# A fused decoder block on one core: inputs of a job in attention split one every two steps, operand of the exchange on VectorE, the last class of keys split at the end of a slot

## The chip, the core and the metric

The kernel runs on one core of one Trainium2 chip, as one program in one launch. The core's engines are TensorE (PE in the profile, its weight loads PEld), VectorE (DVE), ScalarE (ACT), GpSimd (POOL) and SyncE (SP). Each engine executes its own instructions strictly in program order; an instruction that waits holds up all that stand behind it on the same engine. SP and ACT also issue the DMAs, so a DMA that waits for its buffer, too, holds up its queue. The metric is the device time of one execution in microseconds (us): the median of several executions.

## The reference

One layer of a decoder block on a sequence of 2048 tokens with 1024 channels, all in float32:

```python
mod = c_act @ w_mod[l] + b_mod[l]
shift, scale, gate = jnp.split(mod, 3, axis=-1)
h = rms_norm(x, g_norm[l]) * (1.0 + scale[:, None, :]) + shift[:, None, :]
proj = h @ w_in[l]
x_rnn, z_rnn, q, k, v, z_attn, g_r, g_a = jnp.split(proj, IN_SPLITS, axis=-1)
xc = causal_depthwise_conv(x_rnn, conv_w[l], conv_b[l])
hr = rg_lru(xc, w_a[l], b_a[l], w_x[l], b_x[l], lam[l], positions)
y_rnn = (hr * jax.nn.silu(z_rnn)) @ w_out_rnn[l]
qh, kh = apply_partial_rope(q), apply_partial_rope(k)
o = dilated_attention_mixture(qh, kh, vh).reshape(B, S, D_ATTN)
y_attn = (o * jax.nn.silu(z_attn)) @ w_out_attn[l]
merged = sigmoid(g_r + bg_r) * y_rnn + sigmoid(g_a + bg_a) * y_attn
x = rms_norm(x + gate * (merged @ w_o[l]), g_final)
```

The attention has 8 heads of 128 channels. It is evaluated with three causal windows (128 keys at dilation 1, 512 at dilation 4, 2048 at dilation 16) whose results are merged by their softmax denominators.

## The kernel before

Every large product is done in float32 accuracy with three passes of a cheaper type: each operand is **split** into a high part (a copy rounded to the type `fp32r`) and a low part (the rest), and `mm3` issues high x high, high x low and low x high. So each operand costs a copy (`hi_act` on ACT or `hi_dve` on DVE) and a subtraction (`lo_pool` on POOL or `lo_dve` on DVE) before TensorE can use it.

The program goes through these stages; the times are those of the profiled execution.

- **Prologue** (0 to about 57 us): `x` is normalised and turned, 8 MB of `w_mod` are loaded and reduced to shift and scale; then the first products of the values run. Where TensorE would have nothing to do, `idle_matmuls(n)` issues n matmuls on a constant tile (`busy`).
- **Values** of a half of the tokens (`values_half(f, xs)`; for f = 0 to about 124 us, for f = 1 to about 787 us). `wide_values` runs the products of four groups; each call of `next` on it issues a quarter of a group. `store_values` then evicts a finished PSUM tile on ACT (`ev`, L855). Between them, calls of `next(odd)` advance `build_odd`, a generator of twelve steps which makes the split operands `B12`, `B22` and T1 to T4 that the next stage needs (sums on DVE, high parts on ACT, low parts on DVE; `t` and `hx` are its temporaries). How many calls stand where sets the place of these instructions in the queues of ACT and DVE.
- **Strassen stage** of a half (to about 697 us and 1346 us): the other columns of `w_in`, multiplied in seven products (X, Z, W, V, X, Y, V) per pair. The rotated and plain queries and keys are stored in DRAM (`qT`, `kT`; L1160, L1192).
- **Attention** (about 1346 to 1890 us): 16 heads (8 heads for each half of the tokens) in six units each, `ORDER`: class `c` 0 to 3 (the four residues of the positions modulo 4) and window `w` 0 and 1. A unit takes a **slot**. In a slot the program issues, in this order: what is planned at HEAD, the scores of the unit on TensorE, its softmax (minimum on DVE, L1485; exponential on ACT, L1486), what is planned at SOFTMAX, EXCHANGE and WEIGHTS, the transposes of the unit seven slots before, the sums of the one eight slots before, and what is planned at TAIL. Between these, `spend` issues steps of `steps(jobs)`: the output projections (`pj`), which fill TensorE while the softmax chain runs.
- A head's queries and keys are loaded per class (`load_kq`, into `kraw`, 4 buffers) and split into the single tile `KQ` (`split_kq`: `kq`). `window_queries` rearranges the queries (`q`, on POOL). After a head's six units, `gather` puts the softmax minima and sums into `sm` (four ACT instructions, L1638), `exchange` multiplies it by a constant on TensorE (into a PSUM tile with the tag `sc`, as the scores), and `maxima`, `exponentials` and `weights` make from it the scale of each unit. `enlist` holds the slots: class 3 is loaded at the end of slot B - 3 and split at the head of slot B, where B is the first slot of its head.
- A **job** of the filling work multiplies one quarter of the tokens by one output projection, in 64 steps of three matmuls. Its eight inputs are loaded and split by the tables `LOAD_Y` and `SPLIT_Y`, by step x, where steps 8 to 15 are the first eight of the job, each using one input. `split_y` puts the low parts on POOL or DVE (`yl`). The weights `S<-wD` are loaded in the same order on SP. The eight inputs of the first job are split at once before attention.
- **End** (1890 to 2179 us): the remaining jobs, the last product with `w_o`, and the final norm.

Inside `tc.manual_schedule()` the instructions stand in each engine's queue as the code issues them (strassen stage, attention, end, most of the prologue); the values are outside of it and are ordered by the framework's scheduler. A DMA also waits until the DMA eight places before it has landed (each takes one of eight semaphores in turn).

## Time and profile before

| what | value |
| --- | --- |
| median of 3 runs | 2180.11 us (2179.24 to 2183.7) |
| the profiled execution, and its span from first to last instruction | 2180.94 us, 2179.2 us |
| TensorE's idle time over the span | 34.1 us (2179.2 - 2145.1) |
| idle TensorE from 100 to 200 us, and its mean clock there | 3.6 us, 0.97 |
| idle TensorE from 200 to 1300 us | 1.9 us |
| idle TensorE from 1300 to 1900 us | 12.2 us |
| idle TensorE from 2100 us to the end | 10.2 us |

In the profile, `out<-in` names what an instruction writes and reads, and a bracket behind a row says how long the engine was idle before it and what ended this. Two matmuls of 512 columns start 0.23 us apart at full clock. DMA busy is the mean share of the 16 DMA engines.

### The profile page before, as it was taken

The page shows a single profiled execution, that of the slowest core. Times are in us where ns is not written, and L with a number is a line of the kernel's source. Part 1 is how long each engine was busy: PE and PEld are TensorE (multiplying, and loading weights), DVE is VectorE, ACT ScalarE, POOL GpSimd, SP SyncE. Part 2 cuts the span into 40 slices and gives each one's busy share as a digit, 9 for nine tenths or more (in the row PEclk, how much of TensorE's full clock was granted, in tenths as well). Part 3 has the DMA queues.
Part 4 walks back from the last instruction along what each step waited for, and adds up shares of the span by engine and source line. Part 5 has one row for each costly group of instructions (what it writes and reads, how often), then busy time and mean ns, then how long its engine had stood idle before and what let it go on. Part 6 is the DMA issues. An engine that isn't in the chain of part 4 may idle for free.

```text
span 2179.2 us, 32758 instructions
## 1 busy us (share of the span) xinstructions
PE 2145.1 (98%) x10564; PEld 1791.9 (82%) x10564; DVE 1483.5 (68%) x2564; ACT 1313.1 (60%) x2621; POOL 1075.2 (49%) x803
## 2 busy tenths in 40 slices
PE   9999999999999999999999999999999999999998
PEld 6878888888788888888888887888888988878886
DVE  6579877868656535545446584577777777688887
ACT  5648668668644537457447532677888887343333
POOL 1357677667666323223224665456666665200543
PEclk9999999999999999999999999999999999999999
DMA  8457887887655378899996666888887877898552
GB/s 302 141 202 255 281 299 270 288 287 240 174 112 164 110 247 284 291 312 310 322 330 214 164 160 194 287 251 253 279 262 222 259 236 239 291 314 296 179 174 107
DMA packets 426608, 522.98 MB, mean 240 GB/s; under 512 B 104166, under 2 KB 291778, under 8 KB 425412
## 3 DMA queue, kind: packets, MB, share of 16 engines
q1 hardware_dynamic: 391860, 421.06, 61.9%
q10 hardware_dynamic: 34384, 99.78, 12.3%
q8 instruction: 84, 1.38, 0.2%
q14 instruction: 88, 0.72, 0.1%
q0 software_dynamic: 192, 0.05, 0.0%
HBM read 332.02 MB, written 188.75 MB: 239 GB/s over the span
## 4 chain that ended last, share of the span: by engine, by line
PE 59%; DMA 6%; issue 2%; POOL 2%; ACT 2%; DVE 2%; SPq 1%; ACTq 0%; POOLq 0%; DVEq 0%
PE X L151 12%; PE V L151 11%; PE pj L151 10%; PE Z L151 6%; PE W L151 6%; PE Y L151 5%; PE o L151 3%; PE sc L151 3%; DMA S<-wD 1%; PE pg L151 1%; DMA kraw<-kT 1%; PE pT L1570 1%; DMA vraw<-vN 1%; PE pT L1583 1%; DMA R<-yaT 1%
## 5 line engine op out<-in xcount | busy, mean ns | idle before, releaser
L165 POOL TENSOR_TENSOR S<-R,S 128x512 fp32r<-128x512 f32 x192 | 293.2, 1535 | 182.6 <-ACT S L159 89.3
L151 PE MATMUL X<-T,S 128*128 128x512 f32 x1344 | 326.2, 392 | 4.7 <-ACT ev L855 3.6
L151 PE MATMUL pj<-yh,S 128*128 128x512 f32 x896 | 324.5, 403 | 2.3 <-DMA S<-wD 1.6
L151 PE MATMUL V<-T,S 128*128 128x512 f32 x1344 | 324.2, 390 | 0.2 <-DVE ev L454 0.2
L151 PEld LDWEIGHTS X<-T,S 128*128 128x128 f32 x1344 | 253.3, 189 | 59.2 <-ACT ev L855 4.0
L151 PEld LDWEIGHTS V<-T,S 128*128 128x128 f32 x1344 | 252.0, 188 | 53.8 <-DVE ev L454 0.7
L165 POOL TENSOR_TENSOR S<-s,S 128x512 fp32r<-128x512 f32 x116 | 172.2, 1484 | 144.9 <-ACT S L159 105.5
L151 PEld LDWEIGHTS pj<-yh,S 128*128 128x128 f32 x896 | 168.4, 188 | 32.6 <-DVE st L1485 2.0
L151 PE MATMUL pj<-yl,S 128*128 128x512 f32 x448 | 176.2, 393 | 1.9 <-POOL yl L165 1.4
L1486 ACT ACTIVATE pp<-pp,st 128x256 f32<-128x256 f32 (+3 forms) x256 | 133.5, 523 | 52.9 <-DVE st L1485 52.3
L159 ACT ACTIVATE S<-s 128x512 fp32r<-128x512 f32 x124 | 77.4, 624 | 142.7 <-DVE s L284 92.0
L151 PE MATMUL Z<-T,S 128*128 128x512 f32 x672 | 162.0, 390 | 0.0
L151 PE MATMUL Y<-T,S 128*128 128x512 f32 x672 | 161.8, 390 | 0.0
L151 PE MATMUL W<-T,S 128*128 128x512 f32 x672 | 161.6, 389 | 0.0
L159 ACT ACTIVATE S<-R 128x512 fp32r<-128x512 f32 x200 | 121.2, 621 | 60.1 <-issue 20.4
L168 DVE TENSOR_TENSOR ptl<-pT,pth 128x384 fp32r<-128x384 f32 (+1 forms) x160 | 97.8, 628 | 77.3 <-ACT pth L159 75.1
L151 PEld LDWEIGHTS W<-T,S 128*128 128x128 f32 x672 | 126.0, 188 | 26.9 <-issue 0.9
L151 PEld LDWEIGHTS Z<-T,S 128*128 128x128 f32 x672 | 126.1, 188 | 26.2
L151 PEld LDWEIGHTS Y<-T,S 128*128 128x128 f32 x672 | 125.9, 188 | 26.1
L974 DVE SCALAR_TENSOR_TENSOR xc<-xr,par,xc 128x512 f32<-128x512 f32 x96 | 103.6, 1079 | 54.9 <-ACT xc L968 52.7
L165 POOL TENSOR_TENSOR s<-R,s 128x512 fp32r<-128x512 f32 x32 | 44.1, 1378 | 187.8 <-ACT s L159 168.7
L1550 ACT ACTIVATE pp<-pp,M 128x256 f32<-128x256 f32 (+3 forms) x256 | 118.0, 523 | 9.6 <-DVE M L1673 9.6
(417 smaller groups left out, 4902.9 us busy)
## 6 DMA issues: line engine op xcount, KB each, us to landing
sD<-S ACTq DMA_DIRECT2D x140, 512.0 KB, 3.6
S<-sD SPq DMA_DIRECT2D x140, 512.0 KB, 5.0
S<-wD SPq DMA_DIRECT2D x82, 512.0 KB, 5.6
R<-in_w_in_dram SPq DMA_DIRECT2D x144, 256.0 KB, 3.6
wD<-s ACTq DMA_DIRECT2D x64, 256.0 KB, 5.1
T<-in_w_mod_dram SPq DMA_DIRECT2D x16, 512.0 KB, 8.9
vN<-ev SPq DMA_DIRECT2D x32, 256.0 KB, 2.7
zaT<-ev SPq DMA_DIRECT2D x32, 256.0 KB, 4.4
```

The lines of the kernel that those rows point to most:

```text
L151: nc.tensor.matmul(o, lhsT=l, rhs=r, start=st, stop=sp, **kw)
L159: nc.scalar.activation(o, i, AF.Copy)
L165: nc.gpsimd.tensor_tensor(o, i, h.bitcast(F32), ALU.subtract)
L168: return nc.vector.tensor_tensor(o, i, h.bitcast(F32), ALU.subtract).ins
L974: nc.vector.scalar_tensor_tensor(xc, xr[:, i : i + CH], cw(i), xc, ALU.mult, ALU.add)
L1486: nc.scalar.activation(pdst, pdst, AF.Exp, bias=m_, scale=-1.0, accum_out=l_)
L1550: nc.scalar.activation(pp, pp, AF.Copy, scale=w)
L1570: nc.tensor.transpose(pt[:, c0 + j * P : c0 + (j + 1) * P], pp[i][:, k * P : (k + 1) * P], ident)
L1583: nc.tensor.transpose(pt[:, c * P : (c + 1) * P], pp[:, half * P : (half + 1) * P], ident)
```

## The change

The change has seven parts.

1. The scratch tensors `qT` and `kT` become one, `kqT`, in which the queries of a half lie beside the keys that it uses. A class is loaded by one DMA in place of two, and for the first head the classes 1 to 3 are issued by ACT (before: class 3 alone).
2. `gather` is two `tensor_tensor` on DVE, with the mask broadcast, in place of four activations on ACT.
3. Class 3 is loaded one slot earlier and split at WEIGHTS of slot B - 1 in place of HEAD of slot B.
4. `SPLIT_Y` spaces the splits of inputs 1 to 6 by two steps; `LOAD_Y` is moved accordingly.
5. Of the first job's inputs, 6 and 7 have their low parts on DVE.
6. The prologue has seven more idle matmuls.
7. In `values_half` the calls of `next(odd)` stand earlier.

```diff
-    qT = scratch("qT", [D, 4, NB * P])
-    kT = scratch("kT", [D, 4, NB * P])
+    kqT = scratch("kqT", [D, 4, 2 * NB * P])
+    q_column = lambda n: (n if n < 2 else NB + n) * P
+    k_column = lambda n: (2 + n) * P
...
-        idle_matmuls(2)
-        last_sums(0, fill=1)
+        idle_matmuls(4)
+        last_sums(0, fill=2)
         modulation(0)
         hi_k(1)
         sums(1, 2)
         build_x(0)
         lo_k(1)
         turn_x(1)
+        idle_matmuls(3)
...
         for x, _ in enumerate(wide_values(vx, 1, n1, (1, 0), ws)):
-            if x == 0:
+            for _ in range((1, 2, 1, 0)[x]):
                 next(odd)
         with tc.issue_after(last_ev[0]):
             next(odd)
             next(odd)
-        for x, _ in enumerate(wide_values(vx, 0, n1, (0, 1))):
+        for _ in wide_values(vx, 0, n1, (0, 1)):
             next(odd, None)
-            if x == 0:
-                next(odd, None)
...
             self.nk = (self.bk[1] + 1) * P
+            self.q0, self.k0 = (self.nk, 0) if f else (0, 2 * P)
...
-            q0 = self.bk[0] * P
-            queue = nc.scalar if self.f == self.h == 0 and c == 3 else nc.sync
-            queue.dma_start(t[:, : self.nk], kT[rows, c, : self.nk])
-            queue.dma_start(t[:, self.nk : self.nk + 2 * P], qT[rows, c, q0 : q0 + 2 * P])
+            c0, w = self.f * 2 * P, self.nk + 2 * P
+            (nc.scalar if self.f == self.h == 0 and c else nc.sync).dma_start(t[:, :w], kqT[rows, c, c0 : c0 + w])
...
-            for q in range(4):
-                nc.scalar.activation(self.sm[:, :, q], self.st[:].rearrange("p t g b n -> p g t (b n)"), AF.Copy,
-                                     scale=qm[:, q : q + 1])
+            for g in range(2):
+                nc.vector.tensor_tensor(
+                    self.sm[:, g], self.st[:, :, g].rearrange("p t b n -> p t (b n)").unsqueeze(1).broadcast_to([P, 4, 2, 8]),
+                    qm.unsqueeze(2).unsqueeze(3).broadcast_to([P, 4, 2, 8]), ALU.mult)
...
-            for c, (ld, s, place) in enumerate(((5, 2, HEAD), (5, 2, SOFTMAX), (4, 1, HEAD), (3, 0, HEAD))):
+            for c, (ld, s, place) in enumerate(((5, 2, HEAD), (5, 2, SOFTMAX), (4, 1, HEAD), (4, 1, WEIGHTS))):
...
-                (lo_dve if j and k % 2 or j > NB + 1 else lo_pool)(yl[:], t[:], yh[:])
+                (lo_dve if (k % 2 if j else k > 5) or j > NB + 1 else lo_pool)(yl[:], t[:], yh[:])
...
-    LOAD_Y = {-12: [0], -10: [1], -8: [2], -6: [3], -2: [4], 4: [5], 5: [6], 6: [7]}
-    SPLIT_Y = {-3: [0], 3: [1], 4: [2], 5: [3], 7: [4], 10: [5], 11: [6], 12: [7]}
+    LOAD_Y = {-12: [0], -10: [1], -8: [2], -6: [3], -2: [4], 2: [5], 4: [6], 6: [7]}
+    SPLIT_Y = {-3: [0], 1: [1], 3: [2], 5: [3], 7: [4], 9: [5], 11: [6], 12: [7]}
```

What this does to the queues is shown at three places.

**ACT, end of the values of the first half.** The rows stand just ahead of the evictions `ev` of the last group; `T<-hx` and `T<-t` are high parts from `build_odd`, `S` those of the first operands of the strassen stage. Before:

```order
L159 ACTIVATE T_888<-hx_686 128x512
L159 ACTIVATE T_890<-hx_690 128x512
L159 ACTIVATE T_892<-t_206_1164 128x512
L278 DMA sD<-S_222_1246 128x1024
L159 ACTIVATE T_894<-t_197_1115 128x512
L159 ACTIVATE S_228_1262<-R_218_1236 128x512
L159 ACTIVATE S_226_1256<-s_219_1238 128x512
L855 ACTIVATE ev_1178<-W_1024 128x512
L159 ACTIVATE T_888<-hx_687 128x512
L855 ACTIVATE ev_1187<-X_1025 128x512
L159 ACTIVATE T_890<-hx_691 128x512
L855 ACTIVATE ev_1196<-V_1026 128x512
```

and now:

```order
L160 ACTIVATE T_898<-hx_699 128x512
L160 ACTIVATE S_225_1259<-R_217_1240 128x512
L160 ACTIVATE S_223_1254<-s_221_1247 128x512
L160 ACTIVATE T_902<-t_200_1139 128x512
L279 DMA sD<-S_223_1254 128x1024
L160 ACTIVATE S_229_1270<-R_219_1244 128x512
L160 ACTIVATE S_227_1264<-s_220_1246 128x512
L857 ACTIVATE ev_1194<-W_1056 128x512
L857 ACTIVATE ev_1203<-X_1057 128x512
L857 ACTIVATE ev_1212<-V_1058 128x512
L857 ACTIVATE ev_1221<-X_1059 128x512
```

No high part stands between the evictions any more: the last two of `hx` and the last of `t` have moved ahead of them. Behind the eviction of Z that precedes this stretch ACT has eight high parts of `build_odd` where it had thirteen, and DVE has fewer of its sums and low parts left there too.

**SP, start of attention.** The rows are the first head's loads and the weights of the filling work. Before:

```order
L1432 DMA kraw_12128<-kT 128x256
L1433 DMA kraw_12128<-qT 128x256
L1432 DMA kraw_12131<-kT 128x256
L1433 DMA kraw_12131<-qT 128x256
L1432 DMA kraw_12134<-kT 128x256
L1433 DMA kraw_12134<-qT 128x256
L339 DMA S_2258_12149<-wD 128x1024
L339 DMA S_2260_12168<-wD 128x1024
```

and now:

```order
L1432 DMA kraw_12136<-kqT 128x512
L340 DMA S_2259_12153<-wD 128x1024
L340 DMA S_2261_12172<-wD 128x1024
L1779 DMA fg_12183<-grT 128x512
L340 DMA S_2263_12193<-wD 128x1024
```

One load stands ahead of the weights where six stood; the other three are in ACT's queue, behind the high parts `yh<-T` of the first job and ahead of the first `kq<-kraw`.

**ACT, one slot with a gather** (a head of the second half; `pp` are the softmax tiles, `pth` the high parts of the transposed ones). Before:

```order
L1486 ACTIVATE pp_17537,st_17137<-pp_17537,st_17137 128x512
L1638 ACTIVATE sm_17547<-st_17137,cs_60 128x2x16 x4
L159 ACTIVATE pth_17557<-pT_17552 128x512
L159 ACTIVATE pth_17565<-pT_17561 128x384
L1550 ACTIVATE pp_17067<-pp_17067,M_17162 128x384
L1550 ACTIVATE pp_17067<-pp_17067,M_17162 128x512
L159 ACTIVATE vh_17592<-vraw_17451 128x512
L159 ACTIVATE kq_12082<-kraw_17453 128x768
```

and now:

```order
L1485 ACTIVATE pp_17465,st_17069<-pp_17465,st_17069 128x512
L160 ACTIVATE kq_12090<-kraw_17301 128x768
L160 ACTIVATE pth_17485<-pT_17480 128x512
L160 ACTIVATE pth_17493<-pT_17489 128x384
L1550 ACTIVATE pp_17001<-pp_17001,M_17094 128x384
L1550 ACTIVATE pp_17001<-pp_17001,M_17094 128x512
L160 ACTIVATE vh_17520<-vraw_17382 128x512
L1485 ACTIVATE pp_17541,st_17532<-pp_17541,st_17532 128x384
```

The four activations are gone from ACT, and the high part of class 3 stands where they stood. On DVE the two products `sm` stand behind the minima of the last unit and ahead of the low parts `ptl`. On POOL the low part of class 3 now precedes `vh` in the queue, and the copies `q` follow `vh`.

More of the change, by code (lines that the diff above doesn't have):

```diff
@@ L1122, in decoder_block @@
     NT0, NT1 = (4, 5), 3
-    QK = ((2 * D, qT, -SCALE), (3 * D, kT, 1.0))
+    QK = ((2 * D, q_column, -SCALE), (3 * D, k_column, 1.0))
     def scaled(t, ps, u, qs):
@@ L1136, in rotated_pairs, with rotated @@
     def rotated_pairs(qp, f, Ct, St):
-        for base, dstT, qs in QK:
-            def rotated(i, j, ps, u, dstT=dstT, qs=qs):
+        for base, column, qs in QK:
+            def rotated(i, j, ps, u, column=column, qs=qs):
                 n = 2 * f + j
@@ L1159, in store @@
                         r0 = (4 * i + hh) * P
-                        nc.sync.dma_start(dstT[r0 : r0 + 32, :, n * P : (n + 1) * P],
+                        nc.sync.dma_start(kqT[r0 : r0 + 32, :, column(n) : column(n) + P],
                                           v[0][hh * 32 : (hh + 1) * 32, :].rearrange("p (r j) -> p r j", r=4))
@@ L1181, in plain_pairs, with plain @@
     def plain_pairs(f):
-        for base, dstT, qs in QK:
+        for base, column, qs in QK:
             for t in range(0, 6, 2):
-                def plain(i, j, ps, u, t=t, dstT=dstT, qs=qs):
+                def plain(i, j, ps, u, t=t, column=column, qs=qs):
                     n = 2 * f + j
@@ L1191, in store @@
                         for p0, r0, m in cuts[t + i]:
-                            nc.sync.dma_start(dstT[r0 : r0 + m, :, n * P : (n + 1) * P],
+                            nc.sync.dma_start(kqT[r0 : r0 + m, :, column(n) : column(n) + P],
                                               t0[p0 : p0 + m, :].rearrange("p (r j) -> p r j", r=4))
@@ L1444, in window_queries @@
             for l in range(2):
-                src = KQ[:, l, :, self.nk + i * P : self.nk + (i + 1) * P].bitcast(F32)
+                src = KQ[:, l, :, self.q0 + i * P : self.q0 + (i + 1) * P].bitcast(F32)
                 copy = nc.gpsimd if self.f or self.h else nc.vector
@@ L1500, in scores_c @@
                 o0 = P if n == 1 else 0
-                q = slice(self.nk + i * P, self.nk + (i + 1) * P)
-                mm3(ps[:, o0 : o0 + w], KQ[:, 0, r, q], KQ[:, 1, r, q], KQ[:, 0, r, :w], KQ[:, 1, r, :w],
+                q = slice(self.q0 + i * P, self.q0 + (i + 1) * P)
+                ks = slice(self.k0, self.k0 + w)
+                mm3(ps[:, o0 : o0 + w], KQ[:, 0, r, q], KQ[:, 1, r, q], KQ[:, 0, r, ks], KQ[:, 1, r, ks],
                     first=n != 1, last=True, skip_group_check=True)
@@ L1515, in keys @@
         def keys(self, l, w0, nb):
-            ap = KQ[:, l, 0, w0 * 32 : w0 * 32 + 32]
+            ap = KQ[:, l, 0, self.k0 + w0 * 32 : self.k0 + w0 * 32 + 32]
             return bass.AP(ap.tensor, ap.offset, [list(ap.ap[0]), [32, nb], [KQW, 4], [1, 32]])
```

## The prediction

> **What bounds the kernel now.** I read the page's busy line first, then the busy times by stage, then TensorE's waits, then the timeline at the longest of them.
>
> ```profile
> PE 2145.1 (98%) x10564; PEld 1791.9 (82%) x10564; DVE 1483.5 (68%) x2564; ACT 1313.1 (60%) x2621; POOL 1075.2 (49%) x803
> ...
> 20.00:24.00 4.00, 4.00 (x11) 3.17 (x12) 3.96 (x7) 2.55 (x4) 0.00 (x0) 0.57 1.08 362
> 126.00:133.00 7.00, 5.23 (x12) 4.14 (x13) 6.06 (x7) 3.74 (x7) 3.38 (x2) 0.53 0.43 135
> 1346.00:1370.00 24.00, 21.45 (x102) 16.80 (x101) 8.49 (x26) 8.04 (x22) 7.94 (x7) 1.00 0.95 293
> 1370.00:1620.00 250.00, 245.91 (x1596) 217.28 (x1595) 175.16 (x557) 198.46 (x612) 152.44 (x148) 1.00 0.85 265
> 1620.00:1890.00 270.00, 264.81 (x1707) 235.87 (x1705) 195.34 (x470) 211.09 (x515) 156.55 (x121) 1.00 0.77 242
> ```
>
> TensorE is busy for 98% and sets the time; the change takes no matmul from it. So what there is to gain is its idle time, and the time at a low clock. The stage rows give the stretch, then the busy time of PE, PEld, DVE, ACT and POOL, the granted clock, DMA share and GB/s. The clock is about one half in two stretches alone. In attention TensorE idles 2.55 us at the start and 4.09 + 5.19 = 9.3 us behind it. Who ends it (first row: 124 to 1340 us; the others: 1370 to 1890 us; total, times, longest):
>
> ```profile
> PE X L151 <- ACT ev L855: 3.6, 1, 3.6
> ...
> PE sc L151 <- DVE st L1485: 2.3, 3, 1.7
> PE pT L1570 <- ACT pp L1550: 2.1, 6, 0.6
> PE pT L1570 <- DVE ptl L168: 1.4, 2, 0.7
> PE sc L151 <- POOL q L1447: 1.3, 2, 0.8
> PE pj L151 <- POOL yl L165: 0.8, 2, 0.6
> PE pj L151 <- DVE yl L168: 0.5, 1, 0.5
> ```
>
> **Part 7, first half: the eviction that comes late.**
>
> ```profile
> 122.67 1.52 PE L151 MATMUL X<-S,T 128*128 128x512 f32 x6
> 127.77 5.49 PE L151 MATMUL X<-T,S 128*128 128x512 f32 x12 [3.59 <-ACT ev L855]
> 135.90 2.88 PE L151 MATMUL W<-T,S 128*128 128x512 f32 x12
> ...
> 126.60 0.63 ACT L159 ACTIVATE T<-hx 128x512 fp32r<-128x512 f32 x1 [1.46 <-DVE hx L612]
> 104.52 0.60 ACT L855 ACTIVATE ev<-Z 128x512 f32<-128x512 f32 x1 [0.82 <-DMA vN<-ev]
> ...
> 105.67 0.69 DVE L168 TENSOR_TENSOR T<-hx,T 128x512 fp32r<-128x512 f32 x1 [19.04 <-ACT T L159]
> 111.52 1.78 DVE L283 TENSOR_TENSOR s<-R,R 128x512 f32<-128x512 f32 x1
> 131.06 0.68 DVE L619 TENSOR_TENSOR t<-t,T 128x512 f32<-128x512 f32 x1
> ...
> 108.05 4.70 POOL L165 TENSOR_TENSOR S<-R,S 128x512 fp32r<-128x512 f32 x3 [2.94 <-PE X L151]
> ```
>
> TensorE ends the values at 124.2 and needs the PSUM tile X; ACT evicts it just ahead of 127.77, behind a high part at 126.60 that waited for DVE. The wait costs 3.59 us, and the twelve matmuls behind it, at half clock, 5.49 us in place of 2.88. Together 3.59 + 2.61 = 6.2 us. The root is DVE's idle time of 19.04 us before 105.67: its next instruction needs a high part that ACT's queue has only behind the eviction at 104.52.
>
> In the new order DVE gets twelve more of its instructions done in that idle time. From there to the last sum that ACT needs ahead of the evictions (`t_200`) stand 16 instructions; before, 30 took from 105.67 to 131.74, 0.87 each (0.68 alone, 1.78 while POOL works). So `t_200` is there at 105.7 + 13.9 = 119.6. If POOL's five low parts up to then (1.57 each by the row, 7.8 us) are all met at 1.78, 4.4 instructions take 7.8 us and the other 11.6, at 0.68, 7.9: 121.4. ACT then has three high parts and two evictions at about 0.55, 2.8 us: X is free at 122.4 to 124.2, no later than TensorE wants it. Late next would be the operands of Z and W, wanted 6 us earlier; their high parts stand ahead of the evictions, and POOL needs 1.57 for each low part. If three of DVE's instructions also wait for their high part (0.63 each, 1.9), 1.9 us of wait are left at the worst; a wait of 1.59 (below) lies in a stretch whose clock is 1.00. Bounds 4.3 and 6.2; I take **5.9**, since the middle case has no wait.
>
> In the second half the calls move too, but the waits row from 124 to 1340 us has one case of `ev` in all, the one above: nothing to gain there. 0, with 0.3 either way.
>
> **Parts 1, 3 and 5 at the start of attention.**
>
> ```profile
> PE pj L151 <- DMA S<-wD: 1.6, 1, 1.6
> PE pj L151 <- POOL yl L165: 0.6, 2, 0.3
> PE sc L151 <- DVE kq L168: 0.4, 1, 0.4
> ...
> 1352.68 0.32 SPq L1432 DMA_DIRECT2D kraw<-kT  x1
> 1356.36 0.80 SPq L339 DMA_DIRECT2D S<-wD  x2
> ...
> 1347.62 5.04 POOL L165 TENSOR_TENSOR yl<-T,yh 128x512 fp32r<-128x512 f32 x4
> 1356.73 0.63 ACT L159 ACTIVATE kq<-kraw 128x512 fp32r<-128x512 f32 x1 [10.34 <-DMA kraw<-qT]
> ...
> DMA to landing us min/median/max: 2.4/4.9/8.2
> ```
>
> The weights are issued at 1356.36 because six loads of the first head stand before them on SP, and the third waits until POOL has read its old tile (1347.62 + 5.04 = 1352.66). With one load ahead of them they go out ahead of 1352, some 5 us earlier: the 1.6 go. With two low parts on DVE, POOL's last ends 2.5 us earlier: 0.6 go. But the first scores need class 0, whose load goes out as before and lands at about 1356.7; TensorE arrives 0.6 earlier and can wait that much longer. So 1.6 is nearly sure, and the other 1.0 mostly is not. ACT's three DMAs now stand ahead of its first `kq`, but their buffers come free 2.5 us before 1352.66, long before 1356.7. The best is all 2.6; at worst class 0 lands 8.2 us after its issue in place of 6.1 (1350.6 to 1356.7), and 2.1 of wait take the place of the 1.6: 0.5 lost. I take **1.8**, near the row of the weights.
>
> The Trainium skill (DMA: Bandwidth & Descriptors, section Queues, rings and completion order) speaks against the move to ACT's queue: each DMA engine takes turns between the queues that have work. By it the 768 KB on ACT's queue share the engines with class 0 on SP; as an estimate by that rule, its 256 KB at the 293 GB/s of this stretch land 0.9 us later, and the term would be 1.6 - 0.9 = 0.7. No row of the run before shows such a pair.
>
> **Parts 2, 3 and 4 in the rest of attention.**
>
> ```profile
> L1638 ACT ACTIVATE sm<-st,cs x64: 304/307/323, 1379.5 to 1839.0; 128x32 f32<-128x32 f32 x64
> L1650 DVE TENSOR_TENSOR xq<-sc,cs x32: 206/215/225, 1382.5 to 1843.8; 128x64 f32<-128x64 f32 x32
> ...
> 1770.13 0.19 ACT L1486 ACTIVATION_READ_ACCUMULATOR pp<-pp,st 128x1 f32 x1
> 1769.04 0.08 DVE L1485 DVE_READ_ACCUMULATOR2_ANT st<- 128x1 f32 x1
> 1770.87 0.69 DVE L168 TENSOR_TENSOR yl<-R,yh 128x512 fp32r<-128x512 f32 x1 [1.75 <-ACT yh L159]
> 1772.20 1.15 DVE L168 TENSOR_TENSOR ptl<-pT,pth 128x512 fp32r<-128x512 f32 x2 [0.64 <-ACT pth L159]
> ...
> 1438.85 0.74 POOL L165 TENSOR_TENSOR vh<-vraw,vh 128x256 fp32r<-128x256 f32 x1 [3.04 <-ACT vh L159]
> ```
>
> Gather: ACT loses 64 instructions of 0.307, four per head; DVE gains 32 of the shape of `xq` (128x64), 0.215 each, 6.9 us in all. In the slot shown DVE idles 1.75 + 0.64 us at that place anyway, waiting for ACT, so I cost it at nothing; without that cover see the third rival. Class 3: POOL idles 3.04 us before `vh`; the low part moves into this idle time and the copies `q` come earlier by its length: both waits on `q` (1.3) go. Splits two steps apart: the waits on `yl` (1.3 together) come where several splits follow each other; I count 1.0. ACT: the high part of class 3 takes the gather's place, so what is relieved is the slot behind it, by 0.6 to 0.8 us ahead of `pth` and `pp`; I count half of the 2.1 and of the 1.4, 1.7. The wait `sc <- st` is for a PSUM tile that DVE's softmax frees: 0. Sum 4.0, less 1.0 for waits that show behind the removed ones. Bounds: 1 us lost, if the work added to DVE (6.9 us) is uncovered for a seventh, and 7 gained, most of the 8.4 listed; I take **3.0**.
>
> The 64 loads saved, the earlier load of class 3 and the doubled row pitch of the scratch (16 KB in place of 8) count nothing: a head has (1839.0 - 1379.5) / 15 = 30.6 us, a slot 5.1, and the classes are loaded three slots ahead of their split, against a landing of 8.2 at most.
>
> **Part 6, the prologue.**
>
> ```profile
> 19.96 0.73 PE L151 MATMUL X<-S,T 128*128 128x512 f32 x2 [0.65 <-ACT T L570]
> 38.26 0.63 ACT L159 ACTIVATE S<-R 128x512 fp32r<-128x512 f32 x1 [4.74 <-DMA R<-in_w_in_dram]
> 39.61 0.73 PE L151 MATMUL X<-S,T 128*128 128x512 f32 x2 [0.31 <-ACT T L570]
> ```
>
> The seven matmuls (about 0.22 us each, 1.5) fill waits of about 1.1 us and delay the products at 19.96 by some 0.3; if they keep the clock up, the stretch of 4 us at 0.57 is spared, 1.7 us. Either way TensorE waits at 39.61 for an ACT queue that waited 4.74 us for a DMA (DMA share 1.08 in the stretch from 20 us), and nothing of the change moves that DMA. So **0**; bounds 0.4 lost and 1.7 gained.
>
> **Sum.** 5.9 + 1.8 + 3.0 + 0 = 10.7 us. The profiled execution took 2180.94 (its span and 1.74 around it), 0.83 above the median: 2180.94 - 10.7 = 2170.2, and 2169.4 from the median of 2180.11. I predict 2169.5.
>
> **Rivals.** *The eviction stays late*: DVE's round trips with ACT still end behind 124 us, and the half clock follows. For it: DVE is on the path to it as before. Against: 14 instructions fewer. 2180.1 - 4.8 = 2175.3.
>
> *Attention's stalls only change place*: the `pp` and `st` waits depend on a chain through DVE, and the change adds to DVE. Against it: the waits on `q` and on bursts have a cause of their own. 2180.1 - 7.7 = 2172.4.
>
> *DVE is held by the gather* (the slower side): `sm` waits in DVE's queue for the last exponential of its head (1770.32, DVE done at 1769.12: 1.2 us) and takes 0.43, and behind it stand the low parts `ptl` that TensorE's sums need. If this 1.63 came onto TensorE's path in all 16 heads: 26.1 us, 2172.4 + 26.1 = 2198.5. It decides as soon as DVE's idle time there is under 1.6 us; against it are the 2.4 us in the slot shown.
>
> *The prologue's gain is kept too*: 2169.4 - 1.7 = 2167.7, if the DMA at 38.26 was not the limit.
>
> **How the numbers follow.** Chances: forecast 0.57, eviction late 0.19, stalls change place 0.14, gather 0.06, prologue 0.04. About 0.2%, 4.4 us, can be told from no change, so faster means under 2175.7. The late eviction is at this bound and goes half to each side: faster 0.57 + 0.09 + 0.14 + 0.04 = 0.84, same 0.10, slower 0.06. Range: the best terms together (6.2 + 2.6 + 7) give 2164.3, the worst (4.3 - 0.5 - 1, and 0.4 lost in the prologue) 2177.7: 2164 to 2178, which leaves out the gather and little else.
>
> **What would show it.** Right: from 120 to 133 us no wait of TensorE on `ev` over 1 us and a clock of 1.00; `S<-wD` issued near 1351 and no wait for it; no waits on `q`; idle TensorE from 1370 to 1890 us near 6 us; the wait at 39.61 longer or as long. Wrong: a half clock near 126 us, DVE idle before `sm` followed by waits `pT <- DVE ptl` or `o <- ptl` in most heads, or a first score held over 1 us by `kq`.

## The result, and the profile after

The changed kernel takes 2183.56 us (median of 14 runs, 2180.21 to 2187.06) against 2180.61 us (14 runs, 2178.74 to 2183.7): the ratio is 1.0015, with an interval of 1.0007 to 1.0022. It is slower by about 3 us, where 2169.5 with a range of 2164 to 2178 was forecast. The profiled execution took 2183.3 us, its span is 2181.5.

First the page's busy line after the change, then the busy times by stage (columns: stretch, length, busy time of PE, PEld, DVE, ACT, POOL, granted clock, DMA share, GB/s).

```profile
PE 2144.6 (98%) x10571; PEld 1793.0 (82%) x10571; DVE 1490.4 (68%) x2598; ACT 1299.3 (60%) x2557; POOL 1075.1 (49%) x801
```

```profile
20.00:24.00 4.00, 4.00 (x21) 3.13 (x19) 3.84 (x6) 2.22 (x4) 0.00 (x0) 1.00 1.08 361
126.00:133.00 7.00, 7.00 (x33) 5.79 (x32) 1.69 (x2) 3.24 (x6) 2.60 (x3) 1.00 0.71 245
1346.00:1370.00 24.00, 19.85 (x87) 15.59 (x86) 9.21 (x27) 7.46 (x20) 4.37 (x3) 0.93 0.83 264
1370.00:1620.00 250.00, 246.42 (x1601) 218.01 (x1600) 179.87 (x575) 190.63 (x578) 153.14 (x148) 1.00 0.86 267
1620.00:1890.00 270.00, 262.28 (x1691) 235.89 (x1690) 196.44 (x484) 205.97 (x486) 155.66 (x120) 0.99 0.76 238
```

The stretch from 126 to 133 us has lost its wait and its half clock, as forecast. But at the start of attention TensorE now idles 4.15 us in place of 2.55, at a clock of 0.93, and in attention 3.58 + 7.72 = 11.3 us in place of 9.3. That alone does not explain a loss: 5.4 us were gained by 133 us. So I followed the same matmul in both traces. The numbers are the starts, in us from the start of the span, as the timelines have them.

| matmul | before | after | difference |
|---|---|---|---|
| first `X<-T,S` behind the values | 127.77 | 124.86 | -2.91 |
| third group `pg<-xh,gh` of the recurrence | 198.55 | 193.24 | -5.31 |
| `X<-T,S` | 242.17 | 239.94 | -2.23 |
| first `pj`, just ahead of attention | 1346.61 | 1344.67 | -1.94 |
| exchange `sc<-sm,msk` of head 1 | 1382.08 | 1383.38 | +1.30 |
| of head 4 | 1465.94 | 1464.76 | -1.18 |
| of head 9 | 1603.84 | 1604.11 | +0.27 |
| of head 14 | 1774.57 | 1780.96 | +6.39 |
| of head 16 | 1841.90 | 1846.53 | +4.63 |

Three places take the gain back: 3.1 us go between 198 and 242 us, 3.2 between the first `pj` and head 1, and 6.1 between heads 9 and 14. Behind head 14 some 4 us come back (6.39 there, 4.63 at head 16, 2.3 at the end of the span): from 1890 us on TensorE waits 3.2 us in all in the run before, 1.5 in this one.

**198 to 242 us.** VectorE's timeline at the start of the recurrence:

```profile
138.60 0.43 DVE L916 TENSOR_SCALAR bigr<-sg 128x512 bf16<-128x512 int32 x1 [5.11 <-DMA sg<-in_positions_dram]
```

VectorE, in its own order, stands for 5.11 us at the load of the position rows; before the change this instruction started at 140.75 behind a wait of 3.15. So its work starts 2.15 us earlier, not 5.35. TensorE runs ahead until it needs results of that chain, and there waits (TensorE's waits, 124 to 1340 us: total, times, longest):

```profile
PE X L152 <- ACT u L385: 2.5, 3, 1.2
PE pg L152 <- POOL xl L166: 0.8, 1, 0.8
```

Up to 400 us that is 1.3 on `u` and 0.8 on `xl`; in the run before TensorE waits for neither there.

**The start of attention.** TensorE's waits from 1346 to 1370 us, and ScalarE's timeline:

```profile
PE sc L152 <- DVE q L1446: 2.1, 1, 2.1
PE pj L152 <- DVE fg L1785: 0.8, 1, 0.8
PE pj L152 <- POOL yl L166: 0.7, 1, 0.7
```

```profile
1349.14 1.79 ACTq L1432 DMA_DIRECT2D kraw<-kqT  x3
1354.81 0.63 ACT L160 ACTIVATE kq<-kraw 128x512 fp32r<-128x512 f32 x1 [10.22 <-DMA kraw<-kqT]
1357.25 0.63 ACT L160 ACTIVATE kq<-kraw 128x512 fp32r<-128x512 f32 x1 [1.81 <-DMA kraw<-kqT]
1358.99 0.63 ACT L160 ACTIVATE kq<-kraw 128x512 fp32r<-128x512 f32 x1 [1.11 <-DMA kraw<-kqT]
1360.53 0.63 ACT L160 ACTIVATE kq<-kraw 128x512 fp32r<-128x512 f32 x1 [0.91 <-DMA kraw<-kqT]
```

The wait on the weights (1.6) is gone; those on `yl` (0.6 before) and `kq` (0.4 before) are not, and one on `fg` is new. The four classes now come one by one, 1.5 to 2.4 us apart, the last at 1360.5; before, three of the four high parts ran back to back from 1357.72. The queries `q` that VectorE copies from them are late, TensorE waits 2.1 for them, and then runs at half clock for some 3.4 us (below). The 1.6 us more of idle time and half of that stretch, 1.7, make up the 3.2.

**Heads 9 to 14.** VectorE's and GpSimd's timelines in one slot:

```profile
1669.70 3.75 DVE L1638 TENSOR_TENSOR sm<-st,cs 128x64 f32<-128x64 f32 x2 [1.29 <-ACT pp L1485]
1673.38 1.14 DVE L169 TENSOR_TENSOR ptl<-pT,pth 128x512 fp32r<-128x512 f32 x2
```

```profile
1668.46 1.29 POOL L166 TENSOR_TENSOR vh<-vraw,vh 128x512 fp32r<-128x512 f32 x1
1669.72 3.66 POOL L166 TENSOR_TENSOR kq<-kraw,kq 128x768 fp32r<-128x768 f32 x2
1673.33 1.28 POOL L166 TENSOR_TENSOR vh<-vraw,vh 128x512 fp32r<-128x512 f32 x1
```

The gather takes 3.75 us for two instructions that were priced at 0.215 each. It stands as long as GpSimd's two `kq` do, to within 0.1 us: each of its two ends when one of those ends. Over all heads, where GpSimd is idle it takes 0.21 to 0.23, and its longest is 1.94:

```profile
L1638 DVE TENSOR_TENSOR sm<-st,cs x32: 211/283/1944, 1380.8 to 1843.2; 128x64 f32<-128x64 f32 x32
```

The 32 rows add up to 23.5 us, against the 6.9 of the prediction. Behind the gather come `ptl` and the softmax that frees a PSUM tile, and TensorE's exchange waits for that tile (TensorE's waits, 1370 to 1890 us):

```profile
PE sc L152 <- DVE st L1484: 7.6, 5, 2.5
...
PE pT L1570 <- ACT pp L1550: 0.7, 2, 0.4
```

`sc <- st` was 2.3 before. Of the waits that the change was to remove, those on `pp` fell from 2.1 to 0.7 and those on `q` from 1.3 to none; those on `ptl` (1.4 to 1.1) and `yl` (1.3 to 1.1) hardly changed. And three waits over 2 us have a stretch at half clock behind them (busy times by stage, columns as above):

```profile
1362.90:1366.20 3.30, 3.30 (x14) 3.01 (x14) 2.08 (x11) 2.64 (x11) 0.00 (x0) 0.50 0.68 240
1639.40:1642.70 3.30, 3.30 (x13) 2.77 (x12) 2.79 (x11) 2.57 (x7) 1.85 (x3) 0.50 1.10 277
1676.90:1680.20 3.30, 3.30 (x15) 3.01 (x14) 2.35 (x10) 2.98 (x8) 0.00 (x0) 0.50 0.99 343
```

### The profile page after: what moved, and what is told of

It is laid out like the page before. It is cut to its first block, busy times and chain, and to the rows that moved or that the text cites. A ratio compares the mean times of both kernels' runs of the same rounds, so it can differ in the third digit from the quotient of the medians.

```text
span 2181.5 us, 32641 instructions
## 1 busy us (share of the span) xinstructions
PE 2144.6 (98%) x10571; PEld 1793.0 (82%) x10571; DVE 1490.4 (68%) x2598; ACT 1299.3 (60%) x2557; POOL 1075.1 (49%) x801
## 4 chain that ended last, share of the span: by engine, by line
PE 59%; DVE 4%; DMA 4%; ACT 3%; issue 2%; POOL 1%; SPq 0%; ACTq 0%; POOLq 0%; DVEq 0%
PE X L152 11%; PE V L152 11%; PE pj L152 10%; PE Z L152 6%; PE W L152 6%; PE Y L152 5%; PE sc L152 3%; PE o L152 3%; PE pg L152 1%; PE pT L1570 1%; ACT pp L1485 1%; PE pT L1583 1%; DVE sm L1638 1%; DMA S<-wD 1%; ACT pp L1550 1%
## 5 line engine op out<-in xcount | busy, mean ns | idle before, releaser
L166 POOL TENSOR_TENSOR s<-R,s 128x512 fp32r<-128x512 f32 x32 | 43.8, 1370 | 188.2 <-ACT s L160 172.7
```

The costliest lines, as they stand in the source:

```text
L166: nc.gpsimd.tensor_tensor(o, i, h.bitcast(F32), ALU.subtract)
```

## The experiments

Times are medians; the ratio is to runs of the kernel before on the same chip, with its 95% interval. The kernel before itself read 2179.86 to 2180.61 in these comparisons, so rows can differ by 0.7 us for that reason alone.

Part 3 splits class 3 near the end of slot B - 1; before the change it was split at the head of slot B. The text below says "at the end" and "at the head" for these two places. The end of slot B - 1 comes first in the queues, yet "class 3 early" in the expectations means the head of slot B.

| kernel | us | ratio | interval |
|---|---|---|---|
| the change | 2183.56 | 1.0015 | 1.0007 to 1.0022 |
| gather on ScalarE (part 2 undone) | 2188.0 | 1.0033 | 1.002 to 1.0046 |
| class 3 at the head (part 3 undone) | 2179.08 | 0.9997 | 0.9988 to 1.0006 |
| both undone | 2182.06 | 1.0007 | 0.9998 to 1.0016 |
| gather in a form with one tensor operand | 2194.08 | 1.0068 | 1.0056 to 1.0081 |
| class 3: high part at the end, low part at the head | 2179.82 | 1.0001 | 0.9992 to 1.001 |
| first head's classes 1 and 2 loaded on SP | 2181.97 | 1.0015 | 1.0006 to 1.0023 |
| part 7 alone on the kernel before | 2176.47 | 0.9985 | 0.9976 to 0.9994 |
| class 3 at the head, resets later | 2175.44 | 0.9986 | 0.9976 to 0.9996 |
| these two and first loads on SP | 2172.01 | 0.9969 | 0.9958 to 0.998 |
| the same, class 3 at the very end of slot B - 1 | 2172.53 | 0.9968 | 0.9956 to 0.998 |
| part 4 undone | 2183.54 | 1.0017 | 1.0009 to 1.0026 |
| part 6 undone | 2183.33 | 1.0023 | 1.0014 to 1.0032 |
| class 3 at the head, resets later, first loads on SP, part 4 undone | 2168.38 | 0.9948 | 0.9934 to 0.9962 |
| before + part 7 + resets later | 2172.8 | 0.9969 | 0.9957 to 0.998 |
| before + part 7 + resets later + part 2 | 2169.65 | 0.995 | 0.9938 to 0.9963 |

**Which part of the change costs attention its time?** My first theory blamed the gather: it stands still while GpSimd works. The rivals were class 3's high part on ScalarE, and the gather's wait for the last exponential.

```diff
-            for g in range(2):
-                nc.vector.tensor_tensor(self.sm[:, g], ..., ALU.mult)
+            for q in range(4):
+                nc.scalar.activation(self.sm[:, :, q], ..., AF.Copy, scale=qm[:, q : q + 1])
```

> The changed kernel with part 2 alone undone: the gather is four ScalarE activations a head again; the class-3 split stays at the slot's end. Theory A (the gather on VectorE reads two operands from SBUF and stands still while GpSimd works; 32 of them took 23.5 us in the changed kernel, up to 1.94 each, against 0.21 alone): the waits of TensorE sc <- st, 7.6 us from 1370 to 1890 us, fall to under 3 us, the half-clock stretches at 1639 and 1676 us go, and the time is 2183.6 less 5 to 7, 2177 to 2179. Theory B (ScalarE is late because class 3's high part, 0.83, now stands ahead of pth): the st waits stay over 5 us, since ScalarE now has 0.95 of gather and 0.83 of split in the same place; time 2183 to 2186.

Measured: 2188.0, slower than the changed kernel. Both theories fail in their times, and theory A in its waits (TensorE, 1370 to 1890 us; then the VectorE row that ends the longest of them):

```profile
PE sc L152 <- DVE st L1484: 11.6, 6, 6.2
```

```profile
1771.79 8.00 DVE L169 TENSOR_TENSOR yl<-R,yh 128x512 fp32r<-128x512 f32 x1 [1.68 <-ACT yh L160]
```

Without any gather on VectorE, a low part `yl` (0.69 elsewhere) stood for 8.00 us. So it is not the gather as such: another instruction of VectorE with two operands in SBUF suffers in its place. Four of this kernel's five executions took 2187.55 to 2191.09, the fifth 2181.8, less than the changed kernel's median.

```diff
-... (4, 1, HEAD), (4, 1, WEIGHTS) ...
+... (4, 1, HEAD), (3, 0, HEAD) ...
```

> The changed kernel with part 3 alone undone: class 3 is loaded and split a slot later, as before the change; the gather stays on VectorE. Theory A (VectorE and GpSimd in each other's way): GpSimd's 1.85 us low part of class 3 no longer stands beside the gather, so the 32 gathers take less than 23.5 us in sum, but other low parts still meet them: 10 to 16 us, st waits 2 to 5, time 2179 to 2182. Theory B (class 3's high part delays pth on ScalarE): st waits under 3 us whatever the gathers take; time 2177 to 2179. Theory C (the gather only waits in VectorE's queue for the last exponential, my third rival): st waits stay over 6, time 2183 to 2184.

Measured: 2179.08. The `st` waits halve, and the gathers add up to 17.2 us in place of 23.5, somewhat above theory A's window:

```profile
PE sc L152 <- DVE st L1484: 3.7, 3, 2.0
```

The two edits together:

> The changed kernel with parts 2 and 3 undone together. All theories: the rest of attention is as before the change but for the splits two steps apart, so idle TensorE from 1370 to 1890 us near 9 us, no half clock there; what stays of the difference from before is the gain in the values (about 2) and the loss at the start of attention (about 3): 2180 to 2182. If parts 2 and 3 each gave something that the other hid, this is slower than either alone; if theory A holds, it is about as fast as the run with the gather on ScalarE and faster than the changed kernel by 2 to 4.

Measured: 2182.06. Theory A fails here too: by it this is about as fast as the run with the gather on ScalarE, and it is 5.9 faster. With the three runs above the four corners are there: with class 3 at the head the gather on VectorE gains 3.0 (2182.06 to 2179.08), with class 3 at the end 4.4 (2188.0 to 2183.56); class 3 at the end costs 4.5 with the gather on VectorE and 5.9 with it on ScalarE. By the ratios it is 2.2 and 3.9 gained, 3.9 and 5.7 lost. Part 2 gains, part 3 does the harm. The run with the gather on ScalarE has five executions, of which the profiled one holds the stall of 8.00 us, so the two figures that use it say least. The gain of part 2 is about as large as the intervals, but the two pairs agree on its sign.

Is it class 3's high part on ScalarE or its low part on GpSimd? (`high_kq` and `low_kq` are the two lines of `split_kq`.)

```diff
-                at(B - s, place, self.split_kq, c)
+                if place == WEIGHTS:
+                    at(B - 1, WEIGHTS, self.high_kq, c)
+                    at(B, HEAD, self.low_kq, c)
+                else:
+                    at(B - s, place, self.split_kq, c)
```

> The changed kernel, but class 3's high part (ScalarE) stays at the end of the slot and only its low part (GpSimd) goes back to the head of the next slot. Theory A2 (GpSimd's 1.85 us low part there lengthens a burst of GpSimd work in which VectorE's two-operand instructions get no turn; the run with the gather on ScalarE shows one such yl of 8.00 us): as in the run with class 3 early, st waits under 4.5 us and 2178.5 to 2180.5. Theory B (ScalarE's 0.83 us ahead of pth is what makes VectorE late): as in the changed kernel, st waits near 7.6 and 2182.5 to 2184.5.

Measured: 2179.82, as with all of class 3 at the head; the `st` waits are 4.7, a little over the 4.5 expected. ScalarE's 0.83 us in that place cost nothing that can be measured; GpSimd's low part, 1.85 us, is what costs 3 to 4 us (3.7 by the medians, 3.1 by the ratios).

Does VectorE wait for GpSimd because of its two operands in SBUF?

```diff
-            for g in range(2):
-                nc.vector.tensor_tensor(self.sm[:, g], ..., ALU.mult)
+            for q in range(4):
+                nc.vector.tensor_scalar(self.sm[:, :, q], ..., qm[:, q : q + 1], None, ALU.mult)
```

> The changed kernel with the gather still on VectorE and at the same place, but as four multiplications by a per-partition scalar (one tensor operand in SBUF) in place of two with two tensor operands. Theory A (two SBUF operands make it wait for GpSimd): 64 instructions of 0.15 to 0.25 us, none over 0.5 even where GpSimd works, 10 to 14 us in sum; st waits under 4 us; time 2177 to 2180. Theory C (VectorE's queue and its work are what holds, not GpSimd): more work in the same place, st waits 7 or more; 2183 to 2186. If this form waits for GpSimd too, four waits a head of up to 1.9: 2188 or more.

Measured: 2194.08, the third case. One tensor operand does not help in this form, so it does not take two tensor operands in SBUF to wait for GpSimd; each instruction takes its own turn behind GpSimd, up to 1.897 us, and there are four a head in place of two:

```profile
L1638 DVE TENSOR_SCALAR sm<-st,cs x64: 227/240/1897, 1380.6 to 1853.7; 128x32 f32<-128x32 f32 x64
```

What never waited is `xq`, the row from which the prediction took its price: it has one operand in PSUM, and in the run before its 32 instructions took 0.206 to 0.225 with GpSimd at work beside nearly all of them. That the place of the operands makes the difference is read from these rows; no run moved the gather's operands.

**The start of attention.**

```diff
-(nc.scalar if self.f == self.h == 0 and c else nc.sync).dma_start(...)
+(nc.scalar if self.f == self.h == 0 and c == 3 else nc.sync).dma_start(...)
```

> The changed kernel, but the first head's classes 1 and 2 are loaded on SP's queue ahead of the weights, and only class 3 on ScalarE's, as before the change. Theory D (on ScalarE's queue these loads share the DMA engines with the weights that now go out beside them, and land at 1357.2 to 1360.5 us in place of 1356.7 to 1358.4): classes 1 to 3 land 2 to 3 us earlier in relation to TensorE, the wait on q (2.1) and the half clock behind it (1.7) go, a wait on S<-wD of 0.5 to 1.6 comes back: 1 to 3 us faster than the changed kernel, 2180.5 to 2182.5. Rival (the loads land late because of the rows of the merged scratch, whichever queue): same waits, 2183 to 2184.

Measured: 2181.97. ScalarE's timeline there, and the stretch that was at half clock:

```profile
1354.13 0.63 ACT L160 ACTIVATE kq<-kraw 128x512 fp32r<-128x512 f32 x1 [8.47 <-DMA kraw<-kqT]
1355.48 1.82 ACT L160 ACTIVATE kq<-kraw 128x512 fp32r<-128x512 f32 x3 [0.71 <-DMA kraw<-kqT]
```

```profile
1362.90:1366.20 3.30, 3.30 (x19) 2.84 (x18) 0.81 (x5) 0.99 (x4) 0.00 (x0) 1.00 0.89 274
```

All classes are there by 1356.7 us, where the last of the three high parts starts; TensorE waits 0.7 for `q` and not at all for the weights, and the clock stays up: 4.6 us ahead of the changed kernel at 1366 us. The scratch is merged here too, so it is not its rows. But the run as a whole gains only 1.6: in its profile one gather instruction of 6.09 us at 1664.71, and half clocks near it, took 3.5 us back. What the order of the loads does there is settled by the trace; its worth in the total is not, since 1.6 is within the spread of the runs.

**The values and the recurrence.** Part 7 alone (the change's own edit of `values_half`, as shown with the change) on the kernel before:

> The kernel before with part 7 alone. Theory E (what TensorE gains in the values is in part given back, since VectorE's work in the recurrence starts when the position rows have landed, and they were issued only 1.4 us earlier): TensorE is 5 to 6 us ahead of the kernel before at 135 us and 2 to 2.5 ahead from 245 us on; 2177.5 to 2179. Rival (what was given back came from another part): 5 to 6 us ahead to the end, 2174 to 2176.

Measured: 2176.47. TensorE is 5.66 us ahead at 133 us and 2.55 at 242, by the same matmuls as in the table. VectorE's row at the start of the recurrence is as in the changed kernel:

```profile
138.25 0.43 DVE L914 TENSOR_SCALAR bigr<-sg 128x512 bf16<-128x512 int32 x1 [4.78 <-DMA sg<-in_positions_dram]
```

It ends 1 us under the expectation; in its profile the last products, where nothing of part 7 stands, gained another 2 us.

On SP the load stands behind the stores of the values, and waits for one of them to land. The next kernels put the position tiles elsewhere and write the reset rows behind VectorE's first totals:

```diff
-            t = T(rp, [P, CH], I32, "sg", bufs=2)
+            t = T(rp, [P, CH], I32, "zs", bufs=3)
 ...
-            nc.vector.tensor_scalar(bigr[:, q * CH : (q + 1) * CH], t[:], 0, BIG, ALU.is_equal, ALU.mult)
+            resets.append((bigr[:, q * CH : (q + 1) * CH], t))
 ...
             total(z[:], ps, u)
+            write_resets()
```

> The changed kernel with class 3 split early, and the reset rows of the recurrence written behind VectorE's first totals, from position tiles that lie elsewhere in SBUF, so that their load need not wait for the last store of the values and VectorE does not wait at the head of its queue for it. Theory E: VectorE's idle time of 5.1 us ahead of bigr goes, and TensorE keeps 2 to 3 us more of its 5.4 us: 2179.1 less 2 to 3, 2176 to 2177.5. Rival (the recurrence is bound by the whole of VectorE's and GpSimd's work up to 245 us, not by its start): no gain, 2178.5 to 2179.5.

> The kernel before with part 7 and the later reset rows alone; nothing of parts 1 to 6. Theory E: TensorE keeps some 5 to 6 us from 245 us on in place of 2.5: 2176.5 less 2.5 to 3.5, 2173 to 2174, and GpSimd has its gap of 2.3 us behind the gather, so no execution with the 8 us stall: times within 3 us of each other.

Measured: 2175.44 and 2172.8 (2171.54 to 2175.34, a spread of 3.8 where 3 was expected). The second tells it cleanly, being the kernel before with part 7 and this alone:

```profile
135.74 0.68 DVE L454 TENSOR_TENSOR zs<-V,u 128x512 f32<-128x512 f32 x1
138.87 2.01 DVE L921 TENSOR_SCALAR bigr<-zs 128x512 bf16<-128x512 int32 x2 [2.45 <-DMA zs<-in_positions_dram]
```

The load still waits 2.0 us for a store `vN<-ev` and is there only at 138.87, so the new place of the tile did little, and why the load waits for that store is open. But four more of VectorE's instructions now run ahead of it, and `zs` starts at 135.74 in place of 141.83 with part 7 alone. The matmul that starts at 242.17 in the kernel before starts at 236.18 here, 5.99 earlier, against 2.55 with part 7 alone; at head 1 it is 7.60 against 2.18. The recurrence's late start, not its total of work, took the 3 us.

**The prologue.**

```diff
-        idle_matmuls(4)
-        last_sums(0, fill=2)
+        idle_matmuls(2)
+        last_sums(0, fill=1)
 ...
-        idle_matmuls(3)
```

> The changed kernel with part 6 alone undone (seven idle matmuls fewer in the prologue). Theory (TensorE waits near 40 us for a transfer that nothing of this moves): half clock from about 20.5 to 24 us again, TensorE at the same time within 0.5 us at 41 us and after, 2183 to 2184. Rival (the spared half clock was kept): 1.2 to 1.7 us later from 41 us on, 2184.8 to 2185.3.

Measured: 2183.33, and from 41 to 1355 us TensorE is 0.2 to 0.4 us ahead of the changed kernel: the idle matmuls cost that, and nothing was spared. The half clock did not come back without them:

```profile
20.00:24.00 4.00, 4.00 (x20) 3.33 (x21) 3.96 (x7) 2.58 (x4) 0.00 (x0) 1.00 1.08 362
```

That stretch comes and goes from one execution to the next, with the idle matmuls or without; in the run with class 3 at the head it stood at 30.2 to 33.7 us, and TensorE was back at the same time by 40 us.

**Part 4, and a stall of 8 us.**

The steps of `SPLIT_Y` and `LOAD_Y` as before (the first of them in the diff further below):

> The changed kernel with part 4 alone undone (loads and splits of y at the steps of before). If part 4 gave the 1.0 that was counted for it: waits on yl from 1.1 to 2 or more, 2184 to 2185. If it only moved GpSimd's and VectorE's two-operand work to other slots: within 1 us either way, or faster, 2182 to 2184, with the st waits at other places.

Measured: 2183.54; part 4 gives nothing to the changed kernel. These two kernels put together what gained so far:

> The changed kernel with class 3 split early, the reset rows written later from tiles elsewhere, and the first head's classes 1 and 2 on SP ahead of the weights. If the three act independently: 2175.4 of the run with the first two, less 0 to 2.5 at the start of attention (no half clock there, wait on q under 1 us): 2173 to 2175.5. If the loads at the start no longer matter once TensorE arrives there 3 us earlier: 2175 to 2176.

```diff
-... (4, 1, HEAD), (3, 0, HEAD) ...
+... (4, 1, HEAD), (4, 1, TAIL) ...
```

> As the run beside it, but class 3 keeps its early load and is split at the very end of the slot, behind the sums, in place of the head of the next slot. Theory A2: GpSimd's low part then stands behind the gather and the low parts ptl, the burst of GpSimd is not longer, and the copies q come a little earlier: within 1 us of the run beside it or up to 1.5 faster, 2172 to 2175. Rival (any earlier place puts GpSimd in VectorE's way): st waits over 6 us, 2 to 4 slower.

Measured: 2172.01, 1 us under the expectation, and 2172.53, so class 3 may also stand at the very end of slot B - 1, behind the sums. But their times spread from 2169.55 to 2177.7 and from 2169.33 to 2179.01. The profiled execution of the first has the stall again (VectorE, then GpSimd):

```profile
1761.57 8.02 DVE L169 TENSOR_TENSOR yl<-R,yh 128x512 fp32r<-128x512 f32 x1 [1.68 <-ACT yh L160]
```

```profile
1760.52 1.33 POOL L166 TENSOR_TENSOR vh<-vraw,vh 128x512 fp32r<-128x512 f32 x1
1761.78 1.88 POOL L166 TENSOR_TENSOR kq<-kraw,kq 128x768 fp32r<-128x768 f32 x1
1763.58 1.33 POOL L166 TENSOR_TENSOR yl<-R,yh 128x512 fp32r<-128x512 f32 x1
1764.83 1.34 POOL L166 TENSOR_TENSOR vh<-vraw,vh 128x512 fp32r<-128x512 f32 x1
1766.08 1.85 POOL L166 TENSOR_TENSOR kq<-kraw,kq 128x768 fp32r<-128x768 f32 x1
1767.82 1.21 POOL L1454 CAST q<-kq 128x512 fp32r<-128x512 f32 x2
```

VectorE's `yl` stands until GpSimd's row of instructions runs out. None of these GpSimd rows has an idle time ahead of it; VectorE got no turn between them. In the changed kernel's profile the same `yl`, at 1774.36, got through in 0.81. What may decide it is part 4, which brings a `yh` of ScalarE, and with it GpSimd's `yl`, into this slot early:

```diff
-    SPLIT_Y = {-3: [0], 1: [1], 3: [2], 5: [3], 7: [4], 9: [5], 11: [6], 12: [7]}
+    SPLIT_Y = {-3: [0], 3: [1], 4: [2], 5: [3], 7: [4], 10: [5], 11: [6], 12: [7]}
```

> The fastest combination so far (class 3 early, resets later, first loads on SP) with part 4 undone as well. If part 4's place of the low part yl makes the stall of 8 us possible: no such stall, and times within 3 us of each other, near 2170 to 2172. If it is GpSimd's work without a gap (the gather gone from ScalarE lets yh, vh and kq come earlier): some executions are again 5 to 7 us above the others.

> As the run beside it, with the gather on VectorE (part 2) as the only other change. From the pair with class 3 early (2182.1 with the gather on ScalarE, 2179.1 on VectorE) it gains about 3: 2170 to 2171.5 in most executions. If part 2 alone closes GpSimd's gap, some executions lie 5 to 7 us above these; if that takes part 3 or part 4 too, none does.

Measured: 2168.38 (2167.05 to 2170.71) and 2169.65 (2167.96 to 2169.84), the first 1.6 under what was expected and the second 0.4. No execution lies far above the others, and in the same slot GpSimd has a gap, in which VectorE goes through (GpSimd, then VectorE, of the first):

```profile
1759.51 1.85 POOL L166 TENSOR_TENSOR kq<-kraw,kq 128x768 fp32r<-128x768 f32 x1
1762.54 1.30 POOL L166 TENSOR_TENSOR yl<-R,yh 128x512 fp32r<-128x512 f32 x1 [1.18 <-ACT yh L160]
```

```profile
1761.12 0.79 DVE L169 TENSOR_TENSOR yl<-R,yh 128x512 fp32r<-128x512 f32 x1 [1.46 <-ACT yh L160]
```

So with class 3 at the head the gap is there without part 4 and closed with it, in the executions profiled. The run with class 3 at the head and the resets later, which has part 4, also falls in two groups, seven executions up to 2176.01 and four from 2180.04. The stall also stands in the profiles of two kernels with class 3 at the end: the one with the gather on ScalarE, and the one without part 6 (7.99 us). Five executions each are few for an event that some of them miss; that it cannot happen in these two kernels is not shown.

The second is the simplest kernel that keeps what was good: part 7, the resets and part 2. Both lie 0.5% under the kernel before and more under the change.

## Why the prediction was wrong

**Part 7, 5.9 us forecast.** The gain itself was there as worked out: no wait on `ev` over 0.4 us, a clock of 1.00 from 126 to 133 us, 5.4 us ahead at 133 in the change and 5.7 alone. The step that failed is the one that let it stand to the end: "Late next would be the operands of Z and W". Late next was VectorE's work in the recurrence, whose first instruction waits for a load that stands behind the stores of the values. 3.1 us went there. The row was in the trace before (3.15 us of wait ahead of `bigr` at 140.75), but I looked for the next wait in the stage of the gain and not in the one behind it.

**The start of attention, 1.8 us forecast, 3.2 lost.** The wait on the weights went, as said; the bound of 0.5 lost took only class 0 late. Classes 1 to 3 were set at nothing, since their buffers come free early. But the weights now go out beside them: on ScalarE's queue they were issued at 1349.1 and were there at 1357.2 to 1360.5; with classes 1 and 2 on SP's ahead of the weights, and class 3 alone on ScalarE's, all three were there by 1356.7. The other 1.0 of the best case, mostly not counted, did not come: `yl` (0.7) and `kq` (0.4) still hold TensorE, so part 5, which no run tests alone, shows no gain. The rule cited there from the Trainium skill (DMA: Bandwidth & Descriptors, section Queues, rings and completion order) spoke against this step, and the trace agrees with its sign; the estimate by it of 0.9 us was for class 0 alone. The half clock behind a wait of 2.1 us, some 1.7 us more, was in no term.

**The rest of attention, 3.0 forecast, 3.3 lost.** Two terms failed: class 3, by its sign, and the gather, by its price. *The gather*: "32 of the shape of `xq` (128x64), 0.215 each". Shape was the wrong likeness: `xq` reads PSUM, the gather reads SBUF alone, and it took 23.5 us. The nearest row was in the prediction, "0.68 alone, 1.78 while POOL works", for two operands in SBUF. A rule of the Trainium skill says it in advance (SBUF — State Buffer, section Who interferes with whom): a VectorE instruction with two SBUF inputs contends with a GpSimd instruction that reads SBUF, and the second to come waits for all of the first. The rows of the gather agree; the stalls of 6 to 8 us are longer than that, since several GpSimd instructions went ahead. *Class 3*: "POOL idles 3.04 us before `vh`; the low part moves into this idle time". That row was from the first heads, where class 3's low part takes 1.30; from head 9 on it takes 1.85, and it stood against the gather and `ptl`. It cost some 4 us. The waits on `q` that it was to remove (1.3) are gone as well in the runs with part 2 and class 3 at the head, so it was not needed for them.

Part 2, taken by itself, was right in sign: 3.0 us gained with class 3 at the head, and 3.15 in the last pair of kernels (2172.8 to 2169.65). My third rival, VectorE held by the gather, named the right place, but with the wait for the exponential as its price and in all heads; it is GpSimd's work, in the heads where it coincides. Part 4's 1.0 was not there.

**The prologue, 0 forecast.** Right in time: 0.2 to 0.4 lost, at the lower bound. That idle matmuls keep the clock up there is not shown: without them it stayed up too.

## What to carry to other kernels

Price an instruction that moves to VectorE by a row whose operands lie in the same memories, not by one of the same shape. Here both forms of the gather that read SBUF alone paid for what GpSimd had under way at that moment, once for each instruction. Before work is put into GpSimd's idle time, see who was using the gap: it may be VectorE's only turn. And follow a gain past its own stage to the first instruction of the next, in particular to the load at the head of an in-order queue.

## What the runs showed of the hardware

A VectorE instruction that waits for GpSimd need not get the next turn: it stood through up to seven GpSimd instructions (8.00 us), or through one (up to 1.94). What decides which, these runs do not show: the `yl` that went through in 0.81 us and the one that stood for 8.02 both started some 0.3 us ahead of the end of a GpSimd instruction. Where it went through, GpSimd waited in its turn: its next two `kq` took 4.11 us together, where two take 3.67 elsewhere. The changed kernel without part 6 ran at 2182.55 to 2183.56 in six executions and at 2186.68 to 2189.31 in four; the profiled one, with the stall, is one of the four, and the other three are not profiled.

In the changed kernel, waits of TensorE of 2.1, 2.2 and 2.5 us were each followed within 1.3 us by some 3.4 us at half clock; one of 2.51 us, at 1780.96, was not. At a clock of 0.50 half of that time is lost, so such a stall cost, as an estimate, 1.7 us more than its wait. That the wait brings the half clock on is not shown; the stretch near 20 to 34 us came and went with no wait as long ahead of it.
